# Expert groups: twelve more first products beside routing and gate matrix, and a new order in the spilled groups

## The chip, the cores and the metric

The program runs on one core of a Trainium2 chip. The metric is the device time of one execution in microseconds. Besides the plain executions there is one profiled execution, from which every row below is taken. TensorE multiplies matrices into PSUM, VectorE (DVE) and ScalarE (ACT) do elementwise work, GpSimd (POOL) helps with elementwise work between SBUF tiles, and SyncE (SP) issues the DMAs.

## What is computed

Two transformer blocks over 512 tokens of width 1024, all in float32. The first has three mixers, then a layer of 16384 experts of which every token uses 128 (8 heads, 16 each), then a gated embedding. The second block has linear attention, latent attention and two feed-forward layers. The change lies in the expert layer, cut here to its core:

```python
q = (nf @ w_q).reshape(t, PEER_HEADS, D_KEY)           # 8 heads, two halves of 128
v1, i1 = lax.top_k(s1, TOPK)                           # s1, s2: halves against sub_keys
v2, i2 = lax.top_k(s2, TOPK)
vals, ci = lax.top_k(cand, TOPK)                       # cand: sums of all pairs v1 + v2
idx = (e1 * N_KEYS + e2).reshape(t, PEER_HEADS * TOPK)
gates = jax.nn.softmax(vals, axis=-1)
act = jax.nn.gelu(jnp.einsum("td,tkd->tk", xb, expert_u[idx])) * gates
out = jnp.einsum("tk,tkd->td", act, expert_v[idx])
```

The second block also needs `silu(c) @ ada_w + ada_b`, one vector of 2 x 6 x 1024 numbers for its modulations.

## The kernel before

The activations lie transposed: X is eight tiles of 128 channels by 512 tokens. The expert layer is computed densely. All 16384 experts are taken as 128 **expert tiles** of 128 experts, and a gate matrix that is zero for experts that a token does not use multiplies the activations. Every float32 product is made of three matmuls on a rounded part and a rest (`mm3`, lines 231 to 233): high by high, high by rest, rest by high. The weights arrive as blocks of 1 MB (line 200, three buffers); ScalarE makes the rounded part (line 214) and GpSimd the rest (line 215), both into two buffers, in two halves per block.

An expert tile has a **first product** (`up`, line 611): 8 x 3 matmuls of 512 columns, with a gelu on ScalarE (line 612); a block of weights serves two tiles. Four tiles make a group, 32 groups in all. The **second product** of a group (`down`, lines 634 to 641) makes, for each of the eight tiles of X, 4 x 3 matmuls and an addition to X on VectorE (line 641) that also frees the PSUM bank; there are four such banks. Between them lies `gated` (lines 621 to 632): it loads the group's gates (line 623, 1 MB), multiplies them in (line 627, VectorE), and splits the result into rounded part (line 629, ScalarE) and rest (line 630, VectorE). The split has buffers for two groups, so a group's split waits until the second product of two groups before has ended.

The work goes through three stages:

- **Routing** (`route`): queries, scores, top 16, top 16 of the pairs. TensorE is filled with first products of the first `SPILL` = 60 tiles, handed out by a generator (`spills`, line 615): two for each of 16 score steps (line 697), and 4 before the three transposes near the end (line 773). Each group of four activations is stored to DRAM (`act_d`, line 619).
- **Gate matrix** (`build_g`): 64 steps of 8 tokens. VectorE makes four one-hot products per step (lines 822, 823, 827 twice), at most two steps ahead of their use; TensorE makes 16 small matmuls (line 845), ScalarE copies the result out (line 849), and SP stores it (`g_d`, line 853). Beside 24 of the 64 steps stands one more first product (line 836).
- **Groups** (lines 653 to 665): first the 17 **whole** groups, whose first product is made here, then the 15 **spilled** ones, whose activations are loaded (line 657) into one of two buffers. For each group come, in this order, the first product or the load, `gated`, and the second product of the group before it. Beside the second products run the **row sums** (line 926): 96 products with their sum on VectorE, for the modulation vector, each with a load of 512 KB (line 917, two buffers); `every` says beside which additions, 4 in a whole group's turn and 3 in a spilled one's.

The order on each engine is set by the framework before the run: by its estimate of when inputs are ready, with the order in the program as priority. Instructions can stand far ahead of their place in the text. Only those marked `keep_in_program_order`, the row sums among them, stay behind the VectorE instruction that precedes them in the program. At run time every queue, that of SP included, is worked off in its order.

Of the kernel before, what the change touches and what calls it, by code (L numbers as in the profile page):

```python
# [1 line left out]

# [1 line left out]

# [5 lines left out]
F32 = mybir.dt.float32  # L10
# [11 lines left out]
P = 128  # L22
S = 512
NT = S // P
D = 1024
KD = D // P
# [5 lines left out]
HP = 8  # L32
# [2 lines left out]
NCAND = sum(ROWS)  # L35
E2 = 128
GE = 4
SPILL = 60
ORDER = list(range(SPILL // GE, E2 // GE)) + list(range(SPILL // GE))
TB = 8  # L40
DUP = 4
GB = 32
# [32 lines left out]
class Stream:  # L75
# [4 lines left out]
    def fetch(self, b):  # L80
        if b not in self.raw and b not in self.have:
            self.raw[b] = self.net.load(self.ap[b], self.w, self.loads)
# [40 lines left out]
def run(gen):  # L123
    for _ in gen:
        pass
# [12 lines left out]
class Net:  # L138
# [458 lines left out]
    def peer(self, X, pre=None):  # L597
        nc, tc = self.nc, self.tc
        act_d = self.dp.tile([SPILL // GE, P, GE, S], F32, tag="act_d", name="act_d")
        g_d = self.dp.tile([S // GB, P, E2, GB], F32, tag="g_d", name="g_d")  # L600
        v3 = lambda a: a.rearrange("p (b t) -> p b t", t=GB)
        with self.phase("pk"), ExitStack() as stack:
            ak = stack.enter_context(tc.tile_pool(name="ak", bufs=1, side="right"))
            a4_ = lambda: ak.tile([P, GE, S], F32, tag="a4", name=self.nm("a4"), bufs=2)
            pre = (pre or self.peer_norm(X)).ready()
            ns = pre.hs
            us, vs = Stream(self, "expert_u"), Stream(self, "expert_v")

            def up(gr, a4):
                for j in range(GE):  # L610
                    p = self.proj(us, (gr * GE + j) * KD, ns)
                    nc.scalar.activation(a4[:, j, :], p, AF.Gelu_apprx_tanh)  # L612
                    yield

            def spills():
                for gr in range(SPILL // GE):
                    a4 = a4_()
                    yield from up(gr, a4)
                    nc.sync.dma_start(act_d[gr], a4)

            def gated(gr, a4, pv, ad):
                g4 = ad.tile([P, S // GB, GE, GB], F32, tag="g4", name=self.nm("g4"), bufs=2)
                nc.sync.dma_start(g4, g_d[:, :, gr * GE : (gr + 1) * GE, :].rearrange("b p e t -> p b e t"))
                out = []
                for j in range(GE):
                    a = a4[:, j, :]
                    nc.vector.tensor_tensor(v3(a), v3(a), g4[:, :, j, :], ALU.mult)  # L627
                    h, lo = (pv.tile([P, S], F32R, tag=t, name=self.nm(t), bufs=2 * GE) for t in ("ah", "al"))
                    nc.scalar.copy(h, a)  # L629
                    nc.vector.tensor_tensor(lo, a, h.bitcast(F32), ALU.subtract)  # L630
                    out.append((h, lo))
                return out

            def down(gr, at, As, mods, every):
                for n in range(KD):
                    if n % every == 1:
                        next(mods, None)
                    p = self.ps()
                    for j in range(GE):
                        self.mm3(p, vs.unit((at * KD + n) * GE + j), As[j], j == 0, j == GE - 1)  # L640
                    nc.vector.tensor_tensor(X[n], X[n], p, ALU.add)  # L641

            fill = spills()
            with tc.tile_pool(name="pr", bufs=1) as pr:
                e1T, e2T, gT = self.route(pre, pr, fill)
            with tc.tile_pool(name="pb", bufs=1) as pb:
                self.build_g(pb, e1T, e2T, gT, g_d, fill)
            run(fill)
            with tc.tile_pool(name="ad", bufs=1, side="right") as ad, tc.tile_pool(name="pv", bufs=1) as pv:
                before = None  # L650
                mods = self.ada(ad)
                next(mods)
                for at, gr in enumerate(ORDER):
                    whole = gr * GE >= SPILL
                    if not whole:
                        a4 = a4_()
                        nc.sync.dma_start(a4, act_d[gr])
                    else:
                        a4 = a4_()
                        run(up(gr, a4))  # L660
                    As = gated(gr, a4, pv, ad)
                    if before is not None:
                        down(*before, mods, 2 if whole else 3)
                    before = (gr, at, As)
                down(*before, mods, 3)
                run(mods)

    def route(self, pre, pr, fill):
        nc = self.nc
# [100 lines left out]
        nc.vector.tensor_copy(e1f, e1)  # L770
        e2f = self.g(name="e2f")
        nc.vector.tensor_copy(e2f, e2)
        for _ in range(4):
            next(fill, None)
        outs = []
        for src, dt in ((e1f, F16), (e2f, F16), (vals.rearrange("p t h k -> p (t h k)"), F32)):
# [17 lines left out]
    def build_g(self, pb, e1T, e2T, gT, g_d, fill):  # L794


        nc = self.nc
# [9 lines left out]
        def repeated(src, tag):  # L807
            d = pb.tile([P, S, DUP], F16, tag=tag, name=tag)
            nc.vector.tensor_copy(d, src[:, :, None].to_broadcast([P, S, DUP]))
            return d  # L810

        k1, k2 = repeated(e1T, "k1"), repeated(e2T, "k2")
        parts = repeated(gh, "kh"), repeated(gl, "kl")
# [17 lines left out]
        nxt = hots(0)  # L831
        for t0 in range(0, S, TB):
            o1, og = nxt
            if t0 + TB < S:
                nxt = hots(t0 + TB)
            if t0 // TB * 3 % 8 < 3:
                next(fill, None)
            if t0 % GB == 0:
                gs = pb.tile([P, E2, GB], F32, tag="gs", name=self.nm("gs"), bufs=2)
            for q in range(TB // 4):  # L840
                p = self.ps("gg", 2)
                for i in range(4):
                    t = 4 * q + i
                    for j in range(2):
                        nc.tensor.matmul(  # L845
                            p[:, i * P : (i + 1) * P], o1[:, t, :], og[j][:, t, :], start=(j == 0), stop=(j == 1)
                        )
                r = t0 % GB + 4 * q
                nc.scalar.activation(
                    gs[:, :, r : r + 4], p.rearrange("p (t e) -> p e t", t=4), AF.Copy, scale=1.0 / GSCALE  # L850
                )
            if (t0 + TB) % GB == 0:
                nc.sync.dma_start(g_d[t0 // GB], gs)
# [819 lines left out]
```

## Time and profile before

| | |
|---|---|
| three executions | 3232.93, 3233.8 (median), 3239.72 us |
| profiled execution | 3239.99 us, span 3238.2 us, mean granted clock 0.973 |
| busy share of the span | TensorE 95%, VectorE 59%, GpSimd 45%, ScalarE 33% |
| DMA | 418.59 MB, mean 129 GB/s |

The span runs from the first to the last instruction. A matmul's end is modelled, so a busy TensorE is not TensorE at its peak; "idle before" names the time that an engine stood still ahead of an instruction, and what ended it. The clock is the share of full speed that TensorE was granted.

### The profile page before, as it was taken

Reading aid. Unit: us, or ns where it says so; the run is one execution under the profiler, and the core shown is the slowest. Engines: PE = TensorE matmul, PEld = TensorE weight load, DVE = VectorE, ACT = ScalarE, POOL = GpSimd, SP = SyncE. Lnnn points to the kernel's source line nnn. Section 1 sums busy time; section 2 is a strip of 40 time slices with the busy share of each in tenths; the row PEclk is TensorE's granted clock in tenths of the full one; section 3 lists DMA queues with packets and bytes.
Section 4 is the critical chain, followed back from the end, with each engine's and each line's share of the span. In section 5 each row is a group of like instructions: output and inputs, shape, how many; then the busy total and the mean of one; then the engine's idle time right before and its main releaser. Section 6 shows DMA issues by size and latency. Waiting matters only on the chain.

```text
span 3238.2 us, 38828 instructions
## 1 busy us (share of the span) xinstructions
PE 3064.1 (95%) x15428; PEld 2552.4 (79%) x15428; DVE 1910.5 (59%) x3262; ACT 1056.2 (33%) x1632; POOL 1446.8 (45%) x777
## 2 busy tenths in 40 slices
PE   8599998889999999999999988899999999999998
PEld 7488887677888888887777777678888887888887
DVE  8974778986545555556888556765311267552123
ACT  4232223444332222322222245343322234442222
POOL 5635666222444444444444443533445431244444
PEclk9799999999999999999999998899999999999999
DMA  3122333655544544446776321111222221122321
GB/s 134 71 79 105 117 117 124 234 208 221 185 172 169 182 169 171 167 157 241 255 267 222 107 78 60 65 40 66 91 85 104 98 78 48 53 79 84 117 87 64
DMA packets 131062, 418.59 MB, mean 129 GB/s; under 512 B 7728, under 2 KB 73776, under 8 KB 97088
## 3 DMA queue, kind: packets, MB, share of 16 engines
q1 hardware_dynamic: 130880, 416.11, 36.4%
q8 instruction: 121, 1.98, 0.2%
q14 instruction: 61, 0.50, 0.0%
HBM read 364.70 MB, written 51.38 MB: 128 GB/s over the span
## 4 chain that ended last, share of the span: by engine, by line
PE 67%; DVE 13%; DMA 2%; issue 2%; ACT 1%; POOL 1%; DVEq 0%; POOLq 0%; ACTq 0%
PE mm L231 21%; PE mm L233 20%; PE mm L232 20%; DVE a L627 2%; DMA a<-act_d 2%; DVE al L630 2%; PE gg L845 2%; DVE og L827 1%; DVE o L822 1%; DVE x L641 1%; DVE l L378 1%; PE sm L1223 1%; DVE aw L926 1%; PE sm L1187 1%; DVE sq L295 0%
## 5 line engine op out<-in xcount | busy, mean ns | idle before, releaser
L215 POOL TENSOR_TENSOR wl<-raw,wh 128x1024 fp32r<-128x1024 f32 (+4 forms) x526 | 1261.5, 2421 | 1608.1 <-ACT wh L214 1596.4
L231 PE MATMUL mm<-h,wh 128*128 128x512 f32 (+1 forms) x2524 | 963.5, 382 | 27.0 <-DVE x L964 7.5
L233 PE MATMUL mm<-h,wl 128*128 128x512 f32 (+1 forms) x2524 | 956.6, 380 | 23.6 <-POOL wl L215 23.5
L232 PE MATMUL mm<-l,wh 128*128 128x512 f32 (+1 forms) x2428 | 927.7, 382 | 16.5 <-DVE l L226 12.1
L214 ACT CAST wh<-raw 128x1024 fp32r<-128x1024 f32 (+4 forms) x526 | 509.9, 996 | 1038.8 <-PE mm L232 543.6
L231 PEld LDWEIGHTS mm<-h,wh 128*128 128x128 f32 x2524 | 484.4, 192 | 114.6 <-DVE x L964 8.7
L233 PEld LDWEIGHTS mm<-h,wl 128*128 128x128 f32 x2524 | 483.6, 192 | 113.1 <-POOL wl L215 27.5
L232 PEld LDWEIGHTS mm<-l,wh 128*128 128x128 f32 x2428 | 465.5, 192 | 101.0 <-DVE l L226 12.9
L231 PE MATMUL mm<-ah,wh 128*128 128x512 f32 x1024 | 401.2, 392 | 12.8 <-DVE x L641 12.7
L233 PE MATMUL mm<-ah,wl 128*128 128x512 f32 x1024 | 400.6, 391 | 0.0
L232 PE MATMUL mm<-al,wh 128*128 128x512 f32 x1024 | 400.2, 391 | 0.0
L627 DVE TENSOR_TENSOR a<-a,g 128x512 f32<-128x512 f32 x128 | 189.0, 1498 | 261.7 <-ACT a L612 194.1
L231 PEld LDWEIGHTS mm<-ah,wh 128*128 128x128 f32 x1024 | 193.5, 189 | 56.9 <-issue 14.5
L641 DVE TENSOR_TENSOR x<-x,mm 128x512 f32<-128x512 f32 x256 | 171.0, 679 | 100.4 <-PE mm L233 100.2
L233 PEld LDWEIGHTS mm<-ah,wl 128*128 128x128 f32 x1024 | 193.1, 189 | 40.5
L232 PEld LDWEIGHTS mm<-al,wh 128*128 128x128 f32 x1024 | 193.4, 189 | 40.1
L1472 DVE TENSOR_TENSOR sg<-sg,mm 128x512 f32<-128x512 f32 (+1 forms) x48 | 30.9, 643 | 301.0 <-PE mm L233 288.0
L630 DVE TENSOR_TENSOR al<-a,ah 128x512 fp32r<-128x512 f32 x128 | 176.4, 1394 | 36.5 <-ACT ah L629 34.8
L964 DVE SCALAR_TENSOR_TENSOR x<-mm,mod,x 128x256 f32<-128x256 f32 (+1 forms) x112 | 66.5, 594 | 188.5 <-PE mm L233 188.4
L926 DVE CUSTOM_DVE_ANT_0 aw<-aw,c 128x1024 f32<-128x1024 f32 x96 | 149.5, 1557 | 11.0 <-DMA aw<-in_ada_w 11.0
L629 ACT CAST ah<-a 128x512 fp32r<-128x512 f32 x128 | 79.4, 621 | 220.7 <-PE mm L233 125.4
L231 PE MATMUL mm<-g,wh 128*128 128x512 f32 (+1 forms) x416 | 148.6, 357 | 0.0
(391 smaller groups left out, 3770.0 us busy)
## 6 DMA issues: line engine op xcount, KB each, us to landing
raw<-in_expert_u SPq DMA_DIRECT2D x64, 1024.0 KB, 4.9
raw<-in_expert_v SPq DMA_DIRECT2D x64, 1024.0 KB, 6.9
aw<-in_ada_w SPq DMA_DIRECT2D x96, 512.0 KB, 5.8
raw<-in_ffn_w_in SPq DMA_DIRECT2D x44, 1024.0 KB, 4.8
g_d<-gs SPq DMA_DIRECT2D x16, 2048.0 KB, 7.2
g<-g_d SPq DMA_DIRECT2D x32, 1024.0 KB, 6.4
act_d<-a SPq DMA_DIRECT2D x15, 1024.0 KB, 3.9
a<-act_d SPq DMA_DIRECT2D x15, 1024.0 KB, 4.8
```

Of the source, the lines that this page charges most:

```text
L214: self.keep(nc.scalar.copy(h[:, c], raw[:, c]))
L215: nc.gpsimd.tensor_tensor(lo[:, c], raw[:, c], h[:, c].bitcast(F32), ALU.subtract)
L231: nc.tensor.matmul(out, w[0], x[0], start=start, stop=False)
L232: nc.tensor.matmul(out, w[0], x[1], start=False, stop=False)
L233: nc.tensor.matmul(out, w[1], x[0], start=False, stop=stop)
L627: nc.vector.tensor_tensor(v3(a), v3(a), g4[:, :, j, :], ALU.mult)
L629: nc.scalar.copy(h, a)
L630: nc.vector.tensor_tensor(lo, a, h.bitcast(F32), ALU.subtract)
L641: nc.vector.tensor_tensor(X[n], X[n], p, ALU.add)
L845: nc.tensor.matmul(p[:, i * P : (i + 1) * P], o1[:, t, :], og[j][:, t, :], start=(j == 0), stop=(j == 1))
L926: nc.vector.tensor_tensor_reduce(w, w, c, 1.0, 0.0, ALU.mult, ALU.add, self.mod[:, i : i + 1])
L964: self.nc.vector.scalar_tensor_tensor(x, p, self.mod[:, o + n : o + n + 1], x, ALU.mult, ALU.add)
```

## The change

`SPILL` rises from 60 to 72: 18 groups are spilled and 14 whole, and their order follows (`ORDER`, which also orders the weights of the second product). Of the 72 tiles 37 lie in routing (`IN_ROUTE`: 5 instead of 4 before the transposes) and 35 beside the 64 steps of the gate matrix. In the group stage a new function `fetch` asks for the gates, and for a spilled group's activations, one turn ahead. `gated` becomes a generator that does one tile at a time; `down` advances it after each addition to X. Row sums stand only in the whole groups' turns: one after each of the four tiles of the first product and up to three after the gate products. The last second product comes after the rest of the row sums.

```diff
-SPILL = 60
+SPILL = 72
+IN_ROUTE = 37
@@
-            def gated(gr, a4, pv, ad):
-                g4 = ad.tile([P, S // GB, GE, GB], F32, tag="g4", name=self.nm("g4"), bufs=2)
-                nc.sync.dma_start(g4, g_d[:, :, gr * GE : (gr + 1) * GE, :].rearrange("b p e t -> p b e t"))
-                out = []
+            def gated(a4, g4, As, pv):
                 for j in range(GE):
                     a = a4[:, j, :]
                     nc.vector.tensor_tensor(v3(a), v3(a), g4[:, :, j, :], ALU.mult)
                     h, lo = (pv.tile([P, S], F32R, tag=t, name=self.nm(t), bufs=2 * GE) for t in ("ah", "al"))
                     nc.scalar.copy(h, a)
                     nc.vector.tensor_tensor(lo, a, h.bitcast(F32), ALU.subtract)
-                    out.append((h, lo))
-                return out
+                    As.append((h, lo))
+                    yield
 
-            def down(gr, at, As, mods, every):
+            def down(at, As, beside):
                 for n in range(KD):
-                    if n % every == 1:
-                        next(mods, None)
                     p = self.ps()
                     for j in range(GE):
                         self.mm3(p, vs.unit((at * KD + n) * GE + j), As[j], j == 0, j == GE - 1)
                     nc.vector.tensor_tensor(X[n], X[n], p, ALU.add)
+                    next(beside, None)
+                run(beside)
@@
+                def fetch(at):
+                    if at == len(ORDER):
+                        return None
+                    gr, a4 = ORDER[at], a4_()
+                    if gr * GE < SPILL:
+                        nc.sync.dma_start(a4, act_d[gr])
+                    g4 = ad.tile([P, S // GB, GE, GB], F32, tag="g4", name=self.nm("g4"), bufs=2)
+                    nc.sync.dma_start(g4, g_d[:, :, gr * GE : (gr + 1) * GE, :].rearrange("b p e t -> p b e t"))
+                    return a4, g4
+
                 before = None
                 mods = self.ada(ad)
                 next(mods)
+                nxt = fetch(0)
                 for at, gr in enumerate(ORDER):
-                    whole = gr * GE >= SPILL
-                    if not whole:
-                        a4 = a4_()
-                        nc.sync.dma_start(a4, act_d[gr])
+                    (a4, g4), As = nxt, []
+                    if gr * GE >= SPILL:
+                        for _ in up(gr, a4):
+                            next(mods, None)
+                    nxt = fetch(at + 1)
+                    parts = gated(a4, g4, As, pv)
+                    if gr * GE >= SPILL:
+                        parts = chain(parts, (next(mods, None) for _ in range(KD - GE - 1)))
+                    if before is None:
+                        run(parts)
                     else:
-                        a4 = a4_()
-                        run(up(gr, a4))
-                    As = gated(gr, a4, pv, ad)
-                    if before is not None:
-                        down(*before, mods, 2 if whole else 3)
-                    before = (gr, at, As)
-                down(*before, mods, 3)
+                        down(*before, parts)
+                    before = (at, As)
                 run(mods)
+                down(*before, iter(()))
@@
-        for _ in range(4):
+        for _ in range(IN_ROUTE - 4 * HP):
             next(fill, None)
@@
-            if t0 // TB * 3 % 8 < 3:
+            left = SPILL - IN_ROUTE
+            if t0 // TB * left % (S // TB) < left:
                 next(fill, None)
```

## Rows read from the trace of the kernel before

**Rows 1.** The page's chain of work that ended last, by line.

```profile
PE mm L231 21%; PE mm L233 20%; PE mm L232 20%; DVE a L627 2%; DMA a<-act_d 2%; DVE al L630 2%; PE gg L845 2%; DVE og L827 1%; DVE o L822 1%; DVE x L641 1%; DVE l L378 1%; PE sm L1223 1%; DVE aw L926 1%; PE sm L1187 1%; DVE sq L295 0%
```

**Rows 2.** Busy time by stage: stretch, its length, engines' busy us (instructions), clock, DMA share, GB/s.

```profile
500.00:557.00 57.00, 51.34 (x231) 42.71 (x230) 49.78 (x136) 15.50 (x19) 36.72 (x32) 0.94 0.40 138
557.00:798.00 241.00, 211.07 (x1578) 166.84 (x1577) 210.24 (x257) 103.02 (x175) 65.34 (x24) 0.94 0.53 206
798.00:1498.00 700.00, 700.00 (x3090) 579.60 (x3089) 370.99 (x381) 210.31 (x267) 320.31 (x129) 1.00 0.52 177
1498.00:1850.00 352.00, 339.18 (x1465) 277.23 (x1464) 287.78 (x318) 95.31 (x121) 162.37 (x60) 0.99 0.64 224
```

**Rows 3.** Timeline of TensorE in the gate matrix: start, duration, line, operation, count.

```profile
641.97 0.39 PE L233 MATMUL mm<-h,wl 128*128 128x512 f32 x1
...
645.38 0.39 PE L233 MATMUL mm<-h,wl 128*128 128x512 f32 x1
...
658.81 1.07 PE L845 MATMUL gg<-og,o 128*128 128x128 f16 x16
```

**Rows 4.** Groups by line, 798 to 1477 us: busy us, mean ns, idle before.

```profile
L231 PE MATMUL mm<-h,wh 128*128 128x512 f32 x519 | 201.9, 389 | 0.0
...
L926 DVE CUSTOM_DVE_ANT_0 aw<-aw,c 128x1024 f32<-128x1024 f32 x60 | 94.6, 1577 | 11.0 <-DMA aw<-in_ada_w 11.0
```

**Rows 5.** Timeline of TensorE at the end of routing, with the idle time before.

```profile
544.94 1.12 PE L779 MATMUL sm<-ident,e1f 128*128 128x128 f32 x4 [5.66 <-DVE e1f L770]
```

**Rows 6.** Groups by line, 557 to 798 us.

```profile
L822 DVE TENSOR_TENSOR o<-io,k 128x1024 f16<-128x1024 f16 x64 | 67.8, 1059 | 4.1 <-PE gg L845 3.7
L215 POOL TENSOR_TENSOR wl<-raw,wh 128x1024 fp32r<-128x1024 f32 x24 | 66.2, 2777 | 181.3 <-ACT wh L214 181.3
```

**Rows 7.** Timeline of GpSimd and VectorE beside one block's split, 644 to 656 us.

```profile
646.75 5.60 POOL L215 TENSOR_TENSOR wl<-raw,wh 128x1024 fp32r<-128x1024 f32 x2 [13.87 <-ACT wh L214]
...
647.27 2.88 DVE L822 TENSOR_TENSOR o<-io,k 128x1024 f16<-128x1024 f16 x1
650.07 2.82 DVE L827 TENSOR_TENSOR og<-o,kl 128x1024 f16<-128x1024 f16 x1
...
653.54 0.68 DVE L822 TENSOR_TENSOR o<-io,k 128x1024 f16<-128x1024 f16 x1
654.14 0.69 DVE L827 TENSOR_TENSOR og<-o,kh 128x1024 f16<-128x1024 f16 x1
```

**Rows 8.** Waits, 1498 to 1850 us: who waited for whom, us, times, longest.

```profile
DVE a L627 <- DMA a<-act_d: 37.3, 14, 5.8
...
PE mm L231 <- DVE x L641: 12.7, 8, 2.0
...
SPq L657 <- DVE al L630: 88.7, 14, 12.1
```

**Rows 9.** Timeline of ScalarE: first, then last four of 15 groups' splits.

```profile
1511.34 1.98 ACT L629 CAST ah<-a 128x512 fp32r<-128x512 f32 x3 [7.02 <-PE mm L233]
...
1764.89 2.01 ACT L629 CAST ah<-a 128x512 fp32r<-128x512 f32 x3 [7.59 <-PE mm L233]
...
1790.57 1.99 ACT L629 CAST ah<-a 128x512 fp32r<-128x512 f32 x3 [10.91 <-PE mm L233]
...
1814.60 1.98 ACT L629 CAST ah<-a 128x512 fp32r<-128x512 f32 x3 [9.29 <-PE mm L233]
...
1836.36 1.98 ACT L629 CAST ah<-a 128x512 fp32r<-128x512 f32 x3 [7.02 <-PE mm L233]
```

**Rows 10.** Timeline of VectorE and TensorE: last row sum; around one spilled group's load.

```profile
1763.76 1.22 DVE L926 CUSTOM_DVE_ANT_0 aw<-aw,c 128x1024 f32<-128x1024 f32 x1
...
1804.50 5.67 DVE L627 TENSOR_TENSOR a<-a,g 128x512 f32<-128x512 f32 x2 [5.77 <-DMA a<-act_d]
1810.10 0.68 DVE L641 TENSOR_TENSOR x<-x,mm 128x512 f32<-128x512 f32 x1
...
1810.92 0.47 PE L231 MATMUL mm<-ah,wh 128*128 128x512 f32 x1 [2.03 <-DVE x L641]
```

More of the change, by code (lines that the diff above doesn't have):

```diff
@@ L1 @@
 from contextlib import ExitStack, contextmanager
+from itertools import chain
 import numpy as np
```

## The prediction

> **What bounds the kernel now.** I read the chain of work that ended last first. TensorE's three matmul lines, 231 to 233, make up most of it, and behind them stand the gate product (line 627), its split (line 630), the load of spilled activations and VectorE's four products of the gate matrix [rows 1]. So TensorE is the bound and the question is where it waits. Then I read busy time by stage [rows 2]: the tail of routing (500 to 557 us), the gate matrix (557 to 798), the whole expert groups (798 to 1498), the spilled groups (1498 to 1850). TensorE never stops in the whole groups at full clock. It is idle for 30 of 241 us in the gate matrix, at a clock of 0.94, and 13 of 352 in the spilled groups. The change moves work from the stage without idle time into the one with most, and rewrites the stage with some.
>
> **Prices.** From one matmul of 512 columns to the fifteenth after it takes 3.41 us, 0.2273 each; the 16 small matmuls of one step of the gate matrix (eight tokens, two halves each) take 1.07 us [rows 3]. One expert tile is 8 x 3 matmuls: 24 x 0.2273 = 5.46 us of TensorE.
>
> **Whole groups.** Three groups of four tiles lose their first product here: 12 x 5.46 = 65.5 us less, all of it time, since this line had no idle time before it in its stage [rows 2, 4]. Row sums rise from 4 to 7 per whole group (four beside the first product, three beside the second). Each costs VectorE 1.58 us [rows 4], 4.7 us more per group of 43.6 us (192 matmuls at 0.2273). VectorE is busy 371 of 700 us here, 23.1 us per group, so it comes to 27.8 and I cost this at nothing: the cover is 16 us of spare VectorE time and the four PSUM banks TensorE can run ahead into. What queues behind a row sum that waits for its 512 KB is the next addition to X or gate product; these waits came to 11.0 us in 60 row sums [rows 4]. If the cover were gone, 14 groups would pay up to 4.7 us each; I take 0.
>
> **Routing.** One more tile stands ahead of the three transposes. There TensorE waited 5.66 us for VectorE's first expert index [rows 5]. A tile of 5.46 fits into that hole if its weights are split by then, which no row here shows. The bounds are 0 and 5.5 us; I take +2.
>
> **Gate matrix.** 35 tiles instead of 24 over the same 64 steps, so 17.5 weight blocks of two tiles instead of 12. TensorE's own work was 24 x 5.46 + 64 x 1.07 = 199 us and becomes 35 x 5.46 + 68.5 = 259. VectorE needs four products a step at 0.60 us from start to start [rows 7]: 64 x 2.4 = 154 us. On top comes GpSimd's split of the weights, two instructions per block. While one pair ran, for 5.60 us, VectorE finished two products that took 2.88 and 2.82 us instead of 0.68 each: 4.3 us lost per block [rows 7]. The line means agree: the product on line 822 has a mean of 1059 ns against 680 for an undisturbed one [rows 6, 7]. Before: 154 + 12 x 4.3 = 206 us, and VectorE's row says 210 [rows 2]. So neither engine's sum reaches 241; 31 us, 2.6 per block, are lost because they wait for each other in turn (TensorE runs in order, VectorE has room for two steps of products).
> I size that loss by the stretch between two tiles that holds the GpSimd pair. Before it had 64/24 = 2.67 steps: VectorE 6.4 + 4.3 = 10.7, TensorE 5.46 + 2.85 = 8.3, excess 2.4 per block, against 2.6 measured. After it has 64/35 = 1.83 steps: 4.4 + 4.3 = 8.7 against 5.46 + 1.96 = 7.4, excess 1.3. So 259 + 17.5 x 1.3 = 282 us, **+41**. The bounds are no waits at all (259, +18) and the old 2.6 per block (305, +64).
> The Trainium skill (SBUF — State Buffer, Who interferes with whom) says that of a VectorE instruction with two SBUF inputs and a GpSimd instruction that reads SBUF, the second to issue blocks fully until the first ends. It speaks against adding such splits beside these products. By it the loss is the split's whole duration rather than what the pair above showed; the trace agrees with blocking and puts it at 4.3 of 5.6 us. What full blocking would do is the second rival.
> The three stores of 1 MB and the weights they need hide behind TensorE: DMA is at 0.53 here [rows 2]. On SP's queue a store waits for its fourth tile, and weight loads stand behind it, but three weight buffers cover some 48 us (three blocks at 282/17.5 = 16.1).
>
> **Spilled groups.** 18 instead of 15; the second product itself is not added work (it was done in whole groups). A group's 96 matmuls need 21.8 us. The split of each group starts when TensorE ends the second product of two groups before; from its first start (1511.34) to its fifteenth (1836.36) there are 14 periods of 23.2 us [rows 9]: a loss of 1.4 each, 20 us. Where it comes from: VectorE waits 37.3 us for the loads, and TensorE then 12.7 for additions that stand behind [rows 8]. One case: VectorE waits 5.77 us for the load, does two products, and the addition at 1810.10 releases TensorE after 2.03 us without a bank [rows 10]. The loads themselves wait for the splits that free the buffer [rows 8].
> After the change there are no row sums here (3 x 1.58 us less per group), the products stand behind additions, and the load is asked for one group earlier. But two buffers remain, so the load still can't start before the split of two groups before, and the framework had already put products a group and a half early. I expect the loss per group to fall, not to vanish: 0.5 us, 18 x 0.5 = 9 us, **-11** against 20. Bounds: 0 (-20), and what the groups without row sums show. Two such periods exist, after the last row sum: 25.68 and 24.03 us [rows 9], a loss of 3.1 each, 18 x 3.1 = 56, +36. I stay near the low end, because the first of the two begins while the last row sum (1763.76) still holds up additions [rows 10], and the second waited 5.77 us for its load [rows 10], against a mean of 2.7 (37.3 us in 14 waits, [rows 8]).
>
> **Sum.** -65.5 + 2 + 41 - 11 = -33.5 us. The profiled execution took 3239.99 us, 1.8 more than its span; the median is 3233.8. I apply the sum to the median: **3200 us** (the profiled execution would be near 3206).
>
> **Rivals.**
> Better (0.15): TensorE's work fully covers VectorE in the gate matrix (+18) and no load is waited for (-20): -65.5 + 18 + 0 - 20 = -67, 3166 us. For it: VectorE needs only 231 of 259 us. Against: neither engine reached its sum before.
> GpSimd blocks VectorE wholly (0.12): 2 x 2.78 = 5.6 us per block [rows 6], excess 4.4 + 5.6 - 7.4 = 2.6 per block, 259 + 45 = 304, +45 + 18 = +63. With the rest: -65.5 + 2 + 63 - 11 = -11, 3222 us. For it: both engines stretch. Against: the two products ran inside the pair.
> The rewrite doesn't change the order (0.15): the framework sets each queue from readiness, so moving products in the text does nothing, and the loss stays 1.4 x 18 = 25, +5: -65.5 + 2 + 41 + 5 = -17.5, 3216 us. For it: products already ran early. Against: row sums, which are pinned, are gone.
> Slower (0.13): without row sums in between, each group's products are put right behind the load's issue, VectorE stands still for it and every group loses 3.1 us: -65.5 + 2 + 41 + 36 = +13, 3247 us. Place: VectorE's queue ahead of the third addition of each spilled group. It decides from 2.4 us per group on ((65.5 - 43 + 20) / 18). For it: the two periods. Against: their starts, as told.
>
> **How the numbers follow.** The forecast has 0.45. A measurement of this kernel tells 0.2% (6.5 us) from no change. Faster by more than that: forecast, the better case, 0.13 of the unchanged order and 0.05 of the blocking, 0.78. Within: the rest of these two, 0.09. Slower: 0.13. The range goes from 3168 to 3240: it leaves out the slower case and the end of the better one.
>
> **What would show it.** Matmuls of the first product in the whole groups: 14 x 96 instead of 17 x 96, stage about 65 us shorter. Gate-matrix stage near 282 us with VectorE below 240 busy; 305 would be the blocking. Last row sum before the first spilled split. Period of the spilled splits: 21.8 to 22.3 for the forecast, 23.2 for the unchanged order, 24 and more for the slower case, with the wait for the load ahead of line 627's successor. Wrong would be: TensorE waiting in the whole groups behind row sums, or waiting for split weights in the gate matrix.

## The result and the profile after

| | kernel before | changed kernel |
|---|---|---|
| plain executions, median (lowest to highest) | 3233.4 us (3232.7 to 3239.7) | 3194.2 us (3187.6 to 3199.0) |
| profiled execution, span | 3240.0 us, 3238.2 us | 3196.4 us, 3194.6 us |
| mean granted clock | 0.973 | 0.977 |

The ratio of the times is 0.988, with a 95% interval of 0.986 to 0.990. The change makes the kernel faster by about 39 us; 3200 had been forecast.

I cut both spans at the same three places: the first one-hot product on VectorE, the end of the last small matmul of the gate matrix, and the end of the last addition to X.

| us | before | after | difference | forecast |
|---|---|---|---|---|
| up to the first one-hot product | 557.2 | 558.6 | +1.5 | +2 |
| gate matrix | 238.9 | 269.0 | +30.0 | +41 |
| expert groups | 1086.5 | 1009.7 | -76.8 | -65.5 - 11 = -76.5 |
| the rest of the kernel | 1355.6 | 1357.3 | +1.7 | 0 |

Busy time by stage in the changed kernel (columns as in [rows 2]: stretch, its length, busy us of TensorE, its weight loads, VectorE, ScalarE, GpSimd, then clock, DMA share, GB/s):

```profile
500.00:558.00 58.00, 55.52 (x252) 45.88 (x251) 51.67 (x142) 16.12 (x20) 39.25 (x33) 0.97 0.38 132
558.00:828.00 270.00, 257.72 (x1844) 207.68 (x1843) 237.86 (x257) 117.34 (x197) 98.30 (x35) 0.99 0.56 216
828.00:1396.00 568.00, 565.72 (x2489) 467.87 (x2488) 390.38 (x393) 165.77 (x216) 276.88 (x104) 1.00 0.64 220
1396.00:1837.00 441.00, 437.57 (x1928) 361.18 (x1926) 253.56 (x328) 129.91 (x169) 201.49 (x81) 1.00 0.52 179
```

Two things differ from [rows 2]. The gate matrix leaves TensorE idle for 12 of 270 us instead of 30 of 241, and its clock there is 0.99 instead of 0.94. The spilled groups leave 3 of 441 us idle instead of 13 of 352.

Groups by line in the gate matrix, 558 to 828 us (busy us, mean ns, idle before), and then the row sums' line of the page, over the whole kernel:

```profile
L217 POOL TENSOR_TENSOR wl<-raw,wh 128x1024 fp32r<-128x1024 f32 x35 | 100.4, 2888 | 177.3 <-ACT wh L216 177.3
L837 DVE TENSOR_TENSOR o<-io,k 128x1024 f16<-128x1024 f16 x64 | 78.9, 1232 | 1.6 <-PE gg L861 1.6
L861 PE MATMUL gg<-og,o 128*128 128x128 f16 x1024 | 72.4, 221 | 12.3 <-DVE og L842 11.5
```

```profile
L942 DVE CUSTOM_DVE_ANT_0 aw<-aw,c 128x1024 f32<-128x1024 f32 x96 | 199.6, 2081 | 118.0 <-DMA aw<-in_ada_w 94.8
```

The product that [rows 6] gave with a mean of 1059 ns now has 1232, since more GpSimd splits lie beside it. Yet TensorE waits less. The 96 row sums wait 94.8 us for their weights (11.0 for 60 of them in [rows 4]) and take 2081 ns each instead of 1577.

The spilled groups, seen in ScalarE's splits (the first, then the second and third, the last of 18) and in two rows of the waits from 1396 to 1837 us:

```profile
1418.70 1.99 ACT L629 CAST ah<-a 128x512 fp32r<-128x512 f32 x3 [8.29 <-PE mm L235]
...
1442.91 1.98 ACT L629 CAST ah<-a 128x512 fp32r<-128x512 f32 x3 [9.30 <-PE mm L235]
...
1464.67 1.98 ACT L629 CAST ah<-a 128x512 fp32r<-128x512 f32 x3 [7.02 <-PE mm L235]
...
1791.07 1.98 ACT L629 CAST ah<-a 128x512 fp32r<-128x512 f32 x3 [7.02 <-PE mm L235]
```

```profile
DVE a L627 <- DMA a<-act_d: 47.4, 16, 5.6
...
PE mm L233 <- DVE x L640: 3.0, 2, 2.0
```

After the first period (from one group's first split to the next group's) of 24.2 us every group takes 21.76 us: from 1442.91 to 1791.07 there are 16 periods. That is TensorE's own time for 96 matmuls. VectorE still waits for every load, 47.4 us in 16 waits against 37.3 in [rows 8]. What is gone is the consequence: TensorE waits 3.0 us for additions, not 12.7.

So the time came out within 6 us of the forecast, and the mechanism that I gave for the spilled groups is in doubt: the wait that I wanted to shorten has become longer.

### The profile page after: what moved, and what is told of

It reads as the page before. It is cut to its first block, busy times and chain, and to the rows that moved or that the text cites. A ratio compares the mean times of both kernels' runs of the same rounds, so it can differ in the third digit from the quotient of the medians.

```text
span 3194.6 us, 38906 instructions
## 1 busy us (share of the span) xinstructions
PE 3048.8 (95%) x15428; PEld 2545.1 (80%) x15428; DVE 1905.5 (60%) x3262; ACT 1049.6 (33%) x1632; POOL 1465.6 (46%) x777
## 4 chain that ended last, share of the span: by engine, by line
PE 47%; DVE 5%; issue 1%; ACT 1%; POOL 1%; DVEq 0%; POOLq 0%; ACTq 0%
PE mm L233 15%; PE mm L234 15%; PE mm L235 15%; DVE l L380 1%; PE sm L1239 1%; PE sm L1203 1%; DVE sq L297 0%; DVE m L371 0%; PE gg L1266 0%; PE sm L307 0%; PE gg L1260 0%; DVE x L980 0%; PE mm L1395 0%; PE sm L337 0%; POOL wl L217 0%
## 5 line engine op out<-in xcount | busy, mean ns | idle before, releaser
L217 POOL TENSOR_TENSOR wl<-raw,wh 128x1024 fp32r<-128x1024 f32 (+4 forms) x526 | 1280.2, 2456 | 1544.5 <-ACT wh L216 1537.2
L942 DVE CUSTOM_DVE_ANT_0 aw<-aw,c 128x1024 f32<-128x1024 f32 x96 | 199.6, 2081 | 118.0 <-DMA aw<-in_ada_w 94.8
L627 DVE TENSOR_TENSOR a<-a,g 128x512 f32<-128x512 f32 x128 | 139.8, 1118 | 61.6 <-DMA a<-act_d 47.4
L630 DVE TENSOR_TENSOR al<-a,ah 128x512 fp32r<-128x512 f32 x128 | 141.2, 1109 | 40.7 <-ACT ah L629 39.5
```

The costliest lines, as they stand in the source:

```text
L217: nc.gpsimd.tensor_tensor(lo[:, c], raw[:, c], h[:, c].bitcast(F32), ALU.subtract)
L942: nc.vector.tensor_tensor_reduce(w, w, c, 1.0, 0.0, ALU.mult, ALU.add, self.mod[:, i : i + 1])
```

## The experiments

Theory at this point: moving tiles gives about -34 us, and the rewrite of the groups gives the rest, by taking row sums from between the additions. Rivals: the earlier load does it; or the rewrite does nothing. In the tables, "both stages" is the time from the first one-hot product to the last addition to X: 1325.4 us before, 1278.7 after.

**The tiles alone.** The kernel before, with only the counts changed:

```diff
-SPILL = 60
+SPILL = 72
+IN_ROUTE = 37
@@
-        for _ in range(4):
+        for _ in range(IN_ROUTE - 4 * HP):
@@
-            if t0 // TB * 3 % 8 < 3:
+            left = SPILL - IN_ROUTE
+            if t0 // TB * left % (S // TB) < left:
```

> The kernel before with only the tile counts changed: 72 spilled tiles, 37 in routing, 35 beside the gate matrix; groups, loads and row sums as before. My theory (the tiles give about -65.5 + 1.4 + 30, and the old order of the spilled groups goes on losing 1.4 us in each of 18): 65.5 - 31.4 - 5 = 29 us less than before, about 3204 us, periods of the spilled splits near 23.2 us. Rival (the rewrite of the groups doesn't matter): 3194 us as with the whole change, periods near 21.9.

Measured: 3189.0 us, ratio 0.9865 (0.9843 to 0.9887); both stages 1276.3 us. This is no slower than the whole change, and after a first period of 25.8 us the old order of the groups runs without loss. ScalarE's splits, four in a row and then the last:

```profile
1440.17 2.01 ACT L630 CAST ah<-a 128x512 fp32r<-128x512 f32 x3 [10.93 <-PE mm L234]
...
1461.95 1.98 ACT L630 CAST ah<-a 128x512 fp32r<-128x512 f32 x3 [7.02 <-PE mm L234]
...
1505.47 1.99 ACT L630 CAST ah<-a 128x512 fp32r<-128x512 f32 x3 [7.02 <-PE mm L234]
...
1788.35 1.98 ACT L630 CAST ah<-a 128x512 fp32r<-128x512 f32 x3 [7.02 <-PE mm L234]
```

From 1440.17 to 1788.35 us there are 16 periods of 21.76 us, with row sums between the additions and with loads in the group's own turn. My theory falls here. Then why did the same order lose 1.4 us per group in the kernel before? The timelines show it. GpSimd and VectorE beside one group, in the tiles alone:

```profile
1508.49 5.62 POOL L216 TENSOR_TENSOR wl<-raw,wh 128x1024 fp32r<-128x1024 f32 x2 [4.82 <-ACT wh L215]
1519.34 6.08 POOL L216 TENSOR_TENSOR wl<-raw,wh 128x1024 fp32r<-128x1024 f32 x2 [5.24 <-ACT wh L215]
...
1508.35 3.50 DVE L631 TENSOR_TENSOR al<-a,ah 128x512 fp32r<-128x512 f32 x2
...
1516.73 1.29 DVE L628 TENSOR_TENSOR a<-a,g 128x512 f32<-128x512 f32 x2 [0.93 <-DMA a<-act_d]
1517.94 0.68 DVE L642 TENSOR_TENSOR x<-x,mm 128x512 f32<-128x512 f32 x1
1518.54 1.29 DVE L628 TENSOR_TENSOR a<-a,g 128x512 f32<-128x512 f32 x2
```

And in the kernel before, where the group's splits on ScalarE began at 1558.92 (1505.47 above), with the group ahead of it:

```profile
1548.84 1.29 DVE L627 TENSOR_TENSOR a<-a,g 128x512 f32<-128x512 f32 x2 [1.53 <-DMA a<-act_d]
...
1550.65 3.49 DVE L627 TENSOR_TENSOR a<-a,g 128x512 f32<-128x512 f32 x2
...
1562.16 5.53 DVE L630 TENSOR_TENSOR al<-a,ah 128x512 fp32r<-128x512 f32 x2
...
1572.53 3.51 DVE L627 TENSOR_TENSOR a<-a,g 128x512 f32<-128x512 f32 x2 [2.50 <-DMA a<-act_d]
...
1551.03 5.37 POOL L215 TENSOR_TENSOR wl<-raw,wh 128x1024 fp32r<-128x1024 f32 x2 [5.42 <-ACT wh L214]
1561.93 5.20 POOL L215 TENSOR_TENSOR wl<-raw,wh 128x1024 fp32r<-128x1024 f32 x2 [5.53 <-ACT wh L214]
1572.79 5.51 POOL L215 TENSOR_TENSOR wl<-raw,wh 128x1024 fp32r<-128x1024 f32 x2 [5.66 <-ACT wh L214]
```

The instructions stand in the same order on VectorE in both. What differs is who comes first. In the tiles alone the two `al` start at 1508.35, 0.14 us ahead of GpSimd's pair: the first is done before GpSimd has its turn, and both take 3.50 us. In the kernel before they start at 1562.16, 0.23 us behind GpSimd's pair (1561.93), and take 5.53 us. The buffer is then freed 2 us later, the load is asked for later, and the products meet the next GpSimd pair (1572.79): 3.51 us, where the early order has one product pair behind it and the other under way by then (1.29 us each, the second from 1518.54; GpSimd's pair from 1519.34). Each lateness brings the next. I call these the early and the late order.

The lines at 1548.84 and 1550.65 show how the kernel before gets into the late one. The load of that group took 5.3 us from issue to landing, against 4.7 to 4.8 in its neighbours; the first products waited 1.53 us, not 0.9, so the second pair began at 1550.65, 0.38 us ahead of GpSimd's pair, and was caught by it: 3.49 instead of 1.29 us. The profile of before falls into the late order twice, there and at a load that took 6.5 us (issued at 1703.16), and runs at 21.76 to 21.78 us per group in between.

**Parts of the rewrite, at 72 tiles.** Three kernels take the rewrite apart: the row sums moved, without the rest; the rewrite without the earlier request; the rewrite with the row sums left where they were. The changed signatures of `down` are left out.

```diff
 # row sums moved alone (on top of the tiles alone)
-                        run(up(gr, a4))
+                        for _ in up(gr, a4):
+                            next(mods, None)
@@
-                    if n % every == 1:
-                        next(mods, None)
                     p = self.ps()
@@
+                    if GE <= n < KD - 1:
+                        next(mods, None)
@@
-                        down(*before, mods, 2 if whole else 3)
+                        down(*before, mods if whole else iter(()))
@@
-                down(*before, mods, 3)
                 run(mods)
+                down(*before, iter(()))
```

> As the run before it (tiles alone), and the row sums moved out of the spilled groups into the whole ones (seven in each), while loads and gate products stand in the program as in the kernel before. If the row sums between the additions were what made TensorE wait: periods near 21.9 us, about 3194 us. If the earlier load request is what helps: periods still near 23.2 us, 3204 us. If the slower rival of the prediction holds (without row sums the products move right behind the load): periods of 24 us and more, 3215 us or above.

```diff
 # the changed kernel without the earlier request
-                nxt = fetch(0)
@@
-                    (a4, g4), As = nxt, []
+                    (a4, g4), As = fetch(at), []
@@
-                    nxt = fetch(at + 1)
```

> The changed kernel without the fetch one group ahead: loads of activations and gates are asked for in the group's own turn; row sums in the whole groups alone and products between additions are kept. If the row sums' move is the cause: 3194 us, periods 21.9. If the earlier request is: about 3204 us, periods 23.2, and VectorE waits longer for the loads than the 47 us of the changed kernel.

```diff
 # the changed kernel with the row sums where they were
-                        for _ in up(gr, a4):
-                            next(mods, None)
+                        run(up(gr, a4))
@@
-                    if gr * GE >= SPILL:
-                        parts = chain(parts, (next(mods, None) for _ in range(KD - GE - 1)))
@@
-                        down(*before, parts)
+                        down(*before, parts, 2 if gr * GE >= SPILL else 3)
@@ in down, ahead of each addition's matmuls
+                    if n % every == 1:
+                        next(mods, None)
@@
+                down(*before, iter(()), 3)
                 run(mods)
-                down(*before, iter(()))
```

> The changed kernel with the row sums back where they were before (four in a whole group's turn, three in a spilled one's); the fetch one group ahead and the products between additions are kept. If the row sums' move is the cause: about 3204 us, periods near 23.2 us in the groups that have row sums. If fetch and products are: 3194 us, periods 21.9.

| all with 72 tiles, same chip | ratio to before | both stages | periods of the spilled groups |
|---|---|---|---|
| tiles alone | 0.9865 (0.9843 to 0.9887) | 1276.3 | 21.76, the first 25.8 |
| and row sums moved | 0.9894 (0.9872 to 0.9915) | 1280.7 | 21.76, the first 27.5 |
| changed, no earlier request | 0.9898 (0.9878 to 0.9918) | 1279.7 | 21.76, the first 24.2 |
| changed, row sums as before | 0.9927 (0.9907 to 0.9947) | 1291.2 | 22.99, while row sums last |

The earlier request changes nothing: without it both stages take 1279.7 us, with it 1278.7. Row sums moved alone: the third case of the expectation, products right behind the load and 24 us or more, did not come. In the last kernel the products between additions and the earlier request meet the row sums, and that is the worst of all. Its waits in the spilled groups, 1436 to 1760 us (two views, VectorE's and TensorE's):

```profile
DVE a L627 <- DMA a<-act_d: 82.4, 13, 6.8
...
PE mm L233 <- DVE x L642: 14.4, 15, 1.1
```

The load is waited for 6.3 us per group there (it is issued right behind a row sum's load), and TensorE loses 1.2 us in each. So the rest of the rewrite needs the move of the row sums. Measured against the tiles alone, none of the three kernels gains anything at 72 tiles.

**A late load on purpose.** If the two orders are real, one late load must tip the old code and leave the new one alone. In both kernels the load of the eighth spilled group is made late:

```diff
+                        if gr == 7:
+                            nc.sync.dma_start(a4[:, :1, :], act_d[gr, :, :1, :])
                         nc.sync.dma_start(a4, act_d[gr])
```

> The tiles alone, with one load of spilled activations (the eighth of 18) made late: a quarter of it is loaded first and then the whole, some 2 us later than otherwise. If the old order has two states (products ahead of GpSimd's pair, or behind its start) and only a late load moves it from the one into the other: periods 21.76 up to there, then 22 to 25.7 for several groups, 8 to 20 us more than the tiles alone in the stage. If no such state exists: one longer period, at most 2.5 us in all.

> The changed kernel with the same load made late in the same way. If the order without row sums has enough spare time on VectorE to catch up: at most one period longer than 21.76 us (up to 24), and 21.76 again after it. If the two states are here as well: several long periods, 8 to 20 us more.

The whole load, issued at 1538.80 and 1541.86 us, landed 7.7 and 6.5 us later. That is some 7 and 5 us behind a load in its usual turn (issued 21.76 us behind the one before it, landed 4.8 us later), more than the 2 us that were planned, and less in the changed code. ScalarE's splits around it, first in the old code:

```profile
1528.64 1.99 ACT L630 CAST ah<-a 128x512 fp32r<-128x512 f32 x3 [7.02 <-PE mm L234]
...
1550.40 1.98 ACT L630 CAST ah<-a 128x512 fp32r<-128x512 f32 x3 [7.02 <-PE mm L234]
...
1574.43 1.99 ACT L630 CAST ah<-a 128x512 fp32r<-128x512 f32 x3 [9.29 <-PE mm L234]
...
1598.46 1.98 ACT L630 CAST ah<-a 128x512 fp32r<-128x512 f32 x3 [9.29 <-PE mm L234]
...
1620.68 2.00 ACT L630 CAST ah<-a 128x512 fp32r<-128x512 f32 x3 [7.48 <-PE mm L234]
...
1646.35 1.99 ACT L630 CAST ah<-a 128x512 fp32r<-128x512 f32 x3 [10.91 <-PE mm L234]
```

then in the changed code, with VectorE's products behind the late load:

```profile
1532.62 1.98 ACT L629 CAST ah<-a 128x512 fp32r<-128x512 f32 x3 [7.01 <-PE mm L235]
...
1554.38 1.98 ACT L629 CAST ah<-a 128x512 fp32r<-128x512 f32 x3 [7.02 <-PE mm L235]
...
1576.14 1.98 ACT L629 CAST ah<-a 128x512 fp32r<-128x512 f32 x3 [7.02 <-PE mm L235]
...
1548.41 5.04 DVE L627 TENSOR_TENSOR a<-a,g 128x512 f32<-128x512 f32 x4 [2.18 <-DMA a<-act_d]
```

In the old code four periods of 24.03, 24.03, 22.22 and 25.67 us follow, 8.9 us more than four of 21.76, and then it is back in the early order. In the changed code not one period changes. Its four products meet GpSimd and take 5.04 us, but without row sums VectorE waits some 7 us per group for TensorE and ScalarE alone, and by the next group it has caught up. One reservation: the extra load also led the framework to put all four products of that one turn behind each other (in the old code with one addition between them).

**The rewrite alone, at 60 tiles.** The changed kernel with `SPILL = 60` and `IN_ROUTE = 36`, which gives back the old 24 tiles beside the gate matrix.

> The changed code of the groups alone, with the tile counts of the kernel before (60 spilled, 36 in routing, 24 beside the gate matrix). My theory now: the spilled groups' periods come to 21.76 us (20 us less than in the profiled execution of the kernel before), the whole groups lose about 3 us by row sums between first products, gate matrix unchanged at 239 us: 3233 - 17 = 3216 us. Rival (the groups' code has no part in it): 3229 us, within 0.2% of the kernel before.

Measured: 3225.5 us, ratio 0.9976 (0.9962 to 0.9991). The groups take 1068.2 us, 18 less than in the profile of before, as expected, but the whole kernel gains only some 8 us, between the two cases. In the profiles 11 us are left of the 18: the gate matrix took 2 us more (240.9, at a clock of 0.94 as in [rows 2]), the way to the first one-hot product 3 and the rest of the kernel 2, none of which the rewrite touches. And the profiled execution of before lay 6 us above the median of its kind, this one 3. The spilled groups bear out that the new code takes a late load: the third landed 7.1 us after its issue, and the periods from the first split on are 21.88, 21.79 and 21.76 us.

**GpSimd out of the gate matrix.**

```diff
-            nc.gpsimd.tensor_tensor(lo[:, c], raw[:, c], h[:, c].bitcast(F32), ALU.subtract)
+            if self.alone:
+                nc.scalar.copy(lo[:, c], raw[:, c])
+            else:
+                nc.gpsimd.tensor_tensor(lo[:, c], raw[:, c], h[:, c].bitcast(F32), ALU.subtract)
@@
+                self.alone = True
                 self.build_g(pb, e1T, e2T, gT, g_d, fill)
+                self.alone = False
```

> The changed kernel, but beside the gate matrix GpSimd makes no rests of weights: ScalarE writes a rounded copy into the rest's place instead, so the first products made there lack the third matmul's proper operand (part of the computation is changed). If GpSimd's hold on VectorE is what TensorE waits for: VectorE's products fall back to about 0.65 us each, its busy time in the stage from 238 to about 160 us, and the stage from 269 us to TensorE's own 260 to 262. If TensorE waits for something else (turn of the buffers, weights, clock): the stage stays at 268 us or more.

The stage, 553 to 808 us, by engines and by line:

```profile
553.00:808.00 255.00, 253.63 (x1840) 206.64 (x1839) 167.83 (x257) 146.49 (x228) 6.33 (x3) 1.00 0.59 228
```

```profile
L866 PE MATMUL gg<-og,o 128*128 128x128 f16 x1024 | 70.2, 220 | 1.4 <-DVE og L847 0.7
...
L842 DVE TENSOR_TENSOR o<-io,k 128x1024 f16<-128x1024 f16 x64 | 46.1, 720 | 0.0
```

The gate matrix falls from 269.0 to 253.6 us and TensorE's wait for products from 11.5 to 0.7 us. (The expected 260 counted 35 tiles; one of them runs ahead of the stage, see below.) GpSimd's hold on VectorE is what is left of the loss. Its size: VectorE does the same 257 instructions in 167.8 instead of 237.9 us, while 32 of 35 GpSimd instructions, those of 16 blocks, are gone: 70 / 16 = 4.4 us a block, where the prediction had read 4.3 from a single pair [rows 7].

**Where the row sums cost, and more tiles.** In the changed kernel TensorE waits once in the whole groups, within the first second product of all. VectorE has ten row sums pinned ahead of the first addition to X, which frees a bank (the last of them and what stands behind it, then TensorE):

```profile
882.52 1.21 DVE L942 CUSTOM_DVE_ANT_0 aw<-aw,c 128x1024 f32<-128x1024 f32 x1
883.66 0.68 DVE L640 TENSOR_TENSOR x<-x,mm 128x512 f32<-128x512 f32 x1
884.26 0.68 DVE L630 TENSOR_TENSOR al<-a,ah 128x512 fp32r<-128x512 f32 x1
...
884.39 0.50 PE L233 MATMUL mm<-ah,wh 128*128 128x512 f32 x1 [2.28 <-DVE x L640]
```

The groups of the changed kernel take 3.9 us more than with the tiles alone (1009.7 against 1005.8). The next kernel starts the row sums two groups later, eight to a group; then two kernels have 80 spilled tiles, in the new code (also with eight row sums to a group) and in the old; and the changed kernel runs beside them on the same chip.

```diff
 # row sums from the third whole group on
                         for _ in up(gr, a4):
-                            next(mods, None)
+                            if at > 1:
+                                next(mods, None)
@@
-                    if gr * GE >= SPILL:
-                        parts = chain(parts, (next(mods, None) for _ in range(KD - GE - 1)))
+                    if gr * GE >= SPILL and at > 1:
+                        parts = chain(parts, (next(mods, None) for _ in range(KD - GE)))
```

> The changed kernel, with no row sums in the first two whole groups' turns and eight (instead of seven) in each of the other twelve. If the 4 us that the changed kernel's groups take beyond those of the tiles alone come from the row sums pinned ahead of the first group's splits and additions (TensorE's one wait of 2.28 us and the lower clock after it): 4 us less than the changed kernel, and no wait of TensorE for additions in the whole groups. If eight per turn overfill VectorE: waits of TensorE in later whole groups, same time or more.

```diff
-SPILL = 72
+SPILL = 80
```

> The changed kernel with 80 spilled tiles, 43 of them beside the gate matrix, and eight row sums in each of 12 whole groups. TensorE's work is the same, 43.7 us of it go from the whole groups into the gate matrix. If the gate matrix still has waits to fill (269 us against 260 of its own sum, so 303 for 43 tiles): up to 9 us less than the changed kernel. If about 0.7 us are lost in each block of weights whatever stands beside it (21.5 blocks, 15 us): stage 317 us, the same time as the changed kernel within 5 us.

> The tiles alone (old code of the groups) with 80 spilled tiles. The same two cases as the run before it, for the gate matrix; in the spilled groups 20 periods instead of 18, most at 21.76 us if no load is late, 22 to 25.7 in stretches after a late one.

> The changed kernel once more, for comparison on the same chip as the three runs before it: 3194 us, ratio 0.988 to the kernel before.

| same chip | ratio to before | gate matrix | both stages |
|---|---|---|---|
| changed kernel | 0.9886 (0.9865 to 0.9907) | 268.9 | 1278.5 |
| row sums later | 0.9870 (0.9848 to 0.9893) | 269.9 | 1280.6 |
| 80 tiles, new code | 0.9852 (0.9828 to 0.9875) | 301.8 | 1271.5 |
| 80 tiles, old code | 0.9853 (0.9828 to 0.9878) | 302.1 | 1270.3 |

With the row sums later, the wait in the whole groups is gone, but the profiles show nothing won (groups 1010.7 us, 1009.6 in the changed kernel beside it): the last row sums reach into the first spilled groups, where TensorE's waits for additions grow from 3.0 us (changed kernel, 1384 to 1470 us) to this:

```profile
PE mm L233 <- DVE x L640: 4.9, 3, 2.3
```

The medians, 3195.8 against 3199.3 us, do differ by nearly the 4 us of the expectation, but the intervals overlap widely, and the profile of the changed kernel is that of its fastest execution (3195.2). Whether the move gains anything stays open.

With 80 tiles the gate matrix still had room: its 301.8 us are 42 x 5.46 + 68.5 us (42 of the 43 tiles lie in the stage) and 4 us of waits. TensorE's waits there fall from 11.5 us to a single one of 4.0, in the old code and in the new (new code, stage and wait):

```profile
558.00:870.00 312.00, 307.11 (x2071) 249.94 (x2071) 257.52 (x258) 130.90 (x216) 126.45 (x44) 0.99 0.58 217
```

```profile
PE gg L861 <- DVE og L842: 4.0, 1, 4.0
```

Both stages take 7 to 8 us less than in the changed kernel, and both kernels, at 3189 us, are faster than the changed one beside them (3199 us). The intervals overlap a little; the profiles carry the difference. The old code lost some of it again: its first five periods in the spilled groups took 22.4 to 25.7 us. It came into the late order at the switch from the whole groups, where the second load took 7.3 us (6.9 with the tiles alone); the loads behind it took 4.7 to 4.9. So a late load in the middle of the spilled groups is not the only way into it.

## Why the prediction was right, step by step

**Whole groups, -65.5 us at no price for the row sums.** The removed work came off in full. The price was about 4 us, not 0: one wait of 2.28 us within the first second product, with a fall of the clock behind it, and 1 us more of waits at the transition to the spilled groups (3.0 us; with the tiles alone 2.0). The 4 us are the difference to the tiles alone. The cover that I named was real in the steady groups (row sums there waited 94.8 us for their weights, and TensorE did not wait again before the transition), but it is not there yet at the start, when the row sums beside the first products of two groups stand ahead of the first addition.

**Routing, +2.** It took 1.5 us, which says little: in the other profiles with 37 tiles there the first one-hot product came at 556.3 to 560.2 us (553.6 in the run without GpSimd), against 557.2 in the kernel before.

**Gate matrix, +41, measured +30.** The term was mis-sized, first of all in the waits. I forecast 1.3 us per block after the change, 22.8 us in 17.5 blocks; TensorE waited 11.5 us for products, 0.7 per block. The calibration on the kernel before was sound. I took its 31 us as the stage less VectorE's 210 us and laid the result on TensorE's own work, but TensorE's waits come to nearly the same, 29.5 us or 2.5 per block (waits, 557 to 797 us):

```profile
PE gg L845 <- DVE og L827: 24.4, 16, 3.9
PE gg L845 <- DVE o L822: 5.1, 9, 0.8
```

So the step that missed is the one from there to the denser tiles: the stretch of 8.7 against 7.4 us costs less than their difference. It leaves out that VectorE may be up to two steps ahead when the stretch begins; whether that is the reason was not tried. A second, smaller part: one of the 35 tiles (and one of the 24 before) runs ahead of the first one-hot product, so 5.5 of the 259 us do not lie in the stage. In the run without GpSimd, with hardly a wait and at a clock of 1.00, the stage took 253.6 us, and 34 x 5.46 + 68.5 is 254.1.

The clock I had read in [rows 2] without giving it a price. In the kernel before the granted clock fell eight times in the stage to the lower of its two levels, 0.50 in the trace, for 30.7 us in all, and TensorE was busy for 28.8 us of them: worth up to 14 us, as an estimate (0.94 over 241 us gives the same). My sum for after counts TensorE's work at full clock, and so took these 14 us as given back without a reason. That was luck: one fall is left after the change, worth under 2 us, and none in the run without GpSimd. Idle time gives back 18 us and the clock some 12, together the 30 us by which the added 11 tiles (11 x 5.46 = 60 us) cost less than their own work. In the rows the waits come first: each of the eight falls begins during a wait of TensorE for a product or at most 1.4 us behind one, and so do the eight of the rewrite alone at 60 tiles. No run changed the clock alone.

The rival of whole blocking (3222 us) had the right mechanism and a price counted twice. The pair's 5.6 us hold VectorE's own work as well: a product of 0.68 us beside one GpSimd instruction ends 2.88 us after its start. What is lost is the rest, 2.2 us each, 4.4 per block, nearly the 4.3 that the forecast used.

**Spilled groups, -11, measured -18** (17 periods lose 2.4 us in all, before 14 lost 20). Here the sign was right and the reason wrong. I expected fewer and shorter waits for the loads. They became longer. By the rows the loss of before did not come from the wait itself but from whose turn came first beside GpSimd, and loads late by 0.5 and 1.7 us stand where that changed. TensorE's waits of 12.7 us [rows 8] are the larger part of the 20; behind three of them the clock fell, for 10.2 us in all, worth up to 5 us, and in the changed kernel's spilled groups it did not. The runs with a late load show that the old code has the two orders and that the new one keeps its period; that GpSimd's turn is what tells them apart rests on the rows, since no run took GpSimd out of the spilled groups. With the 3 row sums out of each group VectorE has the spare time to catch up, but which part of the rewrite keeps the period was not tried with a late load. With 72 tiles the old code ran as well in its profile, so at that count the rewrite is worth nothing measurable: 0.9865 for the tiles alone, 0.9882 and 0.9886 for the whole change. At 60 tiles it was worth 8 us. How often the old code falls into the late order, over many executions, one profile of each kernel can't tell; this stays open.

**The rivals.** "The rewrite doesn't change the order" (3216) fell with the periods of 21.76 us. "Slower" (3247) rested on two periods of 25.7 and 24.0 us without row sums; these were the tail of the late order, not what groups without row sums cost. The "better" case (3166) asked for no waits in the gate matrix; 12 us of them are left. (Its 231 us for VectorE are 229 by the forecast's own figures, 154 + 17.5 x 4.3.) The sum missed by 6 us only, because its errors stood against each other: the gate matrix came out 11 us cheaper and the spilled groups 7 us better; the row sums at the start, the transition from whole to spilled groups and the rest of the kernel took some 8 us that I had at nothing (-76.8 + 65.5 + 18 = 6.7 in the groups, and 1.7). What is left is the profiled execution of before, which lay 6 us above its median, that of after 2.

## What to carry to other kernels

Before giving work to a stage with idle time, split what it loses into waits and clock, since the added work may bring the clock back as well. Where VectorE and GpSimd share work, look at which of the two starts first, and by how much: if a few tenths of a microsecond decide, a loss per iteration read from one profile is one of two patterns and not a property of the code. And change one part at a time: the simple part of this change had all of the gain that could be measured at its own tile count.

## What was not expected of the hardware

VectorE's instructions on two SBUF operands and GpSimd's took turns, one instruction each. With VectorE 0.14 us ahead a pair took 3.50 us, with VectorE 0.23 us behind 5.53 us, alone 1.29. The Trainium skill (SBUF — State Buffer, Who interferes with whom) says that issue order and not the shape of the operation decides who blocks; these rows agree, and 4.4 us of VectorE's time per block of weights is what it came to here.

Loads of 1 MB from DRAM landed 4.7 to 5.1 us after their issue in nearly all spilled groups except the first two and the last (up to 7.9 us); single ones of the kernel before took 5.3 and 6.5 us, and where the load was issued 0.4 us behind the 512 KB of a row sum (new code, row sums as before) most took 7.0 to 8.1 us. What held up the single ones is not known.
